# The o projection's four column groups form their products in four ways

## The chip, the cores and the metric

The kernel runs on one core of a Trainium2 chip, as one launch. The metric is the device time of that core in microseconds (us): the median of two runs before the change is 1768.39 us (1767.98 and 1768.80). Lower is better.

## The reference

One layer of a hybrid network works on 128 context tokens and 256 latent tokens, 384 in all, 2048 channels wide. The input projection `h @ w_in` gives q, k, v, an output gate o (1024 channels each), 32 gate columns and a pooling input u. The change touches the product for o alone, and what reads it:

```python
    proj = h @ w_in
    M = MLSTM_WIDTH
    q, k, v, o, g, u = jnp.split(proj, [M, 2 * M, 3 * M, 4 * M, 4 * M + N_GATES * N_HEADS], axis=-1)
    ...
    hm, C, n, m = _mlstm_bidir(q, k, v, gates, C0.astype(f32), n0.astype(f32), m0.astype(f32))
    hm = _rmsnorm(hm, mlstm_norm_w.reshape(N_HEADS, HEAD_DIM)).astype(x.dtype)
    hm = hm.reshape(B, T, M) * jax.nn.sigmoid(o)
    hp = _pool_mixer(u, pool_w, pool_scale, grid_w)
    mix = jnp.concatenate([hm, hp], axis=-1) @ w_out
    x = x + gate_a * _rmsnorm(mix, norm_w[1])
    h = _rmsnorm(x, norm_w[2]) * (1 + scale_f) + shift_f
    y = jnp.square(jax.nn.relu(h @ w1)) @ w2
    x = x + gate_f * _rmsnorm(y, norm_w[3])
```

The conditioning vectors go through a 2048 x 12288 product of their own (adaLN), whose results scale and shift the layers.

## The kernel before

All large products run on TensorE in a rounded 4-byte type, `float32r`, three times each to keep precision. A weight tile is split into a high part `hi` (a copy rounded by ScalarE, L126) and a low part `lo` (the rest, by VectorE, L127), the activations likewise into `xh` and `xl`, and `mm3` (L134 to L137) adds up three products in one PSUM tile: hi with xh, hi with xl, lo with xh. Small products (attention, transposes, adaLN) use plain float32. A PSUM bank is 128 partitions by 512 float32 values, and the kernel has 8 of them, handed out by `bank` (L58).

The program goes through these stages: adaLN for the first norm with the u, v and gate products (up to about 210 us of the profile), the q and k products in four column groups with the attention of one pair of heads behind each, **the o product**, the output projection with `w_out`, and the MLP with `w1` and `w2`, which takes the last 1100 us.

`gemm_T` (L158) forms a transposed product for groups of 256 columns. A group has two PSUM tiles, `acc[g, 0]` and `acc[g, 1]`, of 128 output channels by 384 tokens. The contraction of 2048 runs in four chunks. For each chunk `load_w` starts one 512 KB load from the SP queue and splits it; then come 4 contraction tiles times 2 output tiles times 3 passes, 24 matmuls with 384 tokens as the moving operand and a 128 x 128 weight tile as the stationary one. A group has 96 matmuls. After each chunk the feeds are called: side work in steps, which is a piece of attention (`attention`, L521), of splitting the pooled channels (`split_pool`, L690), or of adaLN on TensorE (`ada1`, `ada_mat`) and on VectorE (`ada2`, `ada_vec`). After the last chunk `evac` reads both PSUM tiles.

For the o product `gemm_T` is called four times, for `w_in` columns 3072, 3328, 3584 and 3840 (L696 to L698), called groups 0 to 3 here. Its `evac_o` (L684) takes the sigmoid of each PSUM tile on ScalarE into a tile named `sig`, and VectorE multiplies the head's output `mix[hd]` by it. The output projection starts right behind, with the groups of columns 0 and 256 sharing four PSUM tiles named `acc_wo`.

The order on each engine comes from a scheduler that keeps the dependences and mostly follows the order of the source. Every matmul instruction comes with a weight load of its own (LDWEIGHTS, engine PEld in the profile). A plain float32 matmul of the source appears as two matmul records in the trace, each with its weight load; a rounded one as one record.

Of the kernel before, what the change touches and what calls it, by code (L numbers as in the profile page):

```python
# [13 lines left out]
P = 128  # L14
D = 2048
KT = D // P
NTOK = 384
NH = 8
M = 1024
# [19 lines left out]
def hymba_kernel(  # L39
# [18 lines left out]
    def bank(name):  # L58
        return psum.tile([P, 512], F32, tag="ps", name=name)

    # ---------------------------------------------------------------- constants and small inputs
    cst = const.tile([P, N_CST, P], F32, name="cst")
# [32 lines left out]

    # silu(c); for every contraction tile in a row of zeros, so that a window of 32 columns puts it in any pair of rows
    cT = const.tile([P, 16, 38], F32, name="cT")
# [7 lines left out]

    # per-channel parameters as columns: prmT [128, 80 | 96]
    prmT = const.tile([P, 176], F32, name="prmT")
# [4 lines left out]

    # ---------------------------------------------------------------- helpers
    def load_w(pieces, name, n=1024, after=(), later=None):
        """pieces: (column offset in the tile view, dram AP [128, a, b]); returns the hi and lo parts."""
        raw = wp.tile([P, 1024], F32, tag="raw", name=f"raw_{name}", bufs=3)
        a = pieces[0][1].shape[1]
        rv = raw[:, 0:n].rearrange("p (a b) -> p a b", a=a)
        for off, src in pieces:
            load_w.ins = nc.sync.dma_start(rv[:, :, off:off + src.shape[2]], src).ins  # L120
        hi = wp.tile([P, 1024], F32R, tag="hi", name=f"hi_{name}", bufs=N_W)
        lo = wp.tile([P, 1024], F32R, tag="lo", name=f"lo_{name}", bufs=N_W)
        with ExitStack() as es:
            for ins in after:
                es.enter_context(tc.issue_after(ins))
            nc.scalar.activation(hi[:, 0:n], raw[:, 0:n], AF.Copy)  # L126
            low = lambda: nc.vector.tensor_tensor(lo[:, 0:n], raw[:, 0:n], hi[:, 0:n].bitcast(F32), op=ALU.subtract)  # L127
            if later is None:
                low()
            else:  # L130
                later.append(low)
        return (hi[:, 0:n].rearrange("p (a b) -> p a b", a=a), lo[:, 0:n].rearrange("p (a b) -> p a b", a=a))

    def mm3(ps, lh, ll, rh, rl, start, stop):  # L134
        nc.tensor.matmul(ps, lh, rh, start=start, stop=False)  # L135
        nc.tensor.matmul(ps, lh, rl, start=False, stop=False)  # L136
        mm3.ins = nc.tensor.matmul(ps, ll, rh, start=False, stop=stop).ins  # L137

    def wview(w):
        return w.rearrange("(k p) n -> p k n", p=P)  # L140

    class Feed:
        """Side work, emitted in steps between the tiles of a large product."""

# [13 lines left out]
    def gemm_T(w, cols, xs, n, evac, feeds=(), korder=(0, 1, 2, 3), name="g", hold=None):  # L158
        """Transposed products: for every 256-column group, out[128 channels, n] in two tiles; groups share the k loop."""
        wv = wview(w)  # L160
        acc = {}
        for g, c0 in enumerate(cols):
            for o in range(2):
                acc[g, o] = bank(f"acc_{name}_{c0}_{o}")
        for ki, kc in enumerate(korder):
            for g, c0 in enumerate(cols):
                hi, lo = load_w([(0, wv[:, 4 * kc:4 * kc + 4, c0:c0 + 256])], f"{name}_{c0}_{kc}", after=hold(ki, g) if hold else ())
                for k in range(4):
                    xh, xl = xs(4 * kc + k)
                    for o in range(2):  # L170
                        mm3(acc[g, o][:, 0:n], hi[:, k, o * P:(o + 1) * P], lo[:, k, o * P:(o + 1) * P],
                            xh[:, 0:n], xl[:, 0:n], ki == 0 and k == 0, ki == 3 and k == 3)
                for f in feeds:
                    f()
        for g, c0 in enumerate(cols):
            for o in range(2):
                evac(c0 // P + o, acc[g, o])
# [7 lines left out]
    def rstd_cols(out, ss, n, scale):  # L185
        """out = (ss * scale + eps) ** -0.5, [128, n]"""
        nc.vector.tensor_scalar(out, ss, scale, EPS, op0=ALU.mult, op1=ALU.add)
        nc.gpsimd.tensor_tensor(out, out, mhalf[:, 0:n], op=ALU.pow)

    def bcast_row(col, name, ps=None):  # L190
        """PSUM tile with [p, 128 i + t] = col[t, i] for every partition p."""
        dg = slot(f"dg_{name}")
        dgv = dg[:, 0:NTOK].rearrange("p (i t) -> p i t", t=P)
        nc.vector.tensor_tensor(dgv, ident.unsqueeze(1).to_broadcast([P, 3, P]), col.unsqueeze(2).to_broadcast([P, 3, P]), op=ALU.mult)
        ps = bank(f"bc_{name}") if ps is None else ps
        nc.tensor.matmul(ps[:, 0:NTOK], ones, dg[:, 0:NTOK], start=True, stop=True)
        return ps

    # ---------------------------------------------------------------- adaLN
    mod = const.tile([P, 6, KT, 2], F32, name="mod")  # L200
    aw = ada_w.rearrange("(p j) n -> p j n", j=16)

    def ada_mat(parts, tags=("ada",)):
        """parts: up to four (i, first channel tile), nk channel tiles each, on the tensor engine.
        Row 32 g + 2 b + (0: ctx, 1: latent) of ps holds part b's sum over the contraction tiles j = g (mod 4)."""
        n, nk = len(parts), parts[0][2]
# [24 lines left out]
    def ada_finish(i, k0, nk, ps):  # L231
        """ps [128, nk, 2]: matrix product columns -> mod[i], with what the channel's norm weight adds to it"""
        v = mod[:, i, k0:k0 + nk, :]
# [10 lines left out]
    def ada_vec(i, q):  # L244
        """512 channels, on the vector engine; the tensor engine adds up the partitions"""
        acc = wp.tile([P, 2, 512], F32, tag="adaacc", name=f"ada_acc_{i}_{q}", bufs=1)
# [27 lines left out]

    # ---------------------------------------------------------------- x: statistics and transposes
    ksteps = [(k, 2) for k in range(0, KT, 2)]
# [45 lines left out]

    # ---------------------------------------------------------------- h, and u, v, gates (token-major), k outermost
    h = []
# [74 lines left out]

    # ---------------------------------------------------------------- pooling mixer  # L400
    mix = [None] * KT
# [22 lines left out]

    # ---------------------------------------------------------------- gate rows, stabilisers
    tokc = ((0, 1, 2), (0, 2, 1))
# [76 lines left out]

    # ---------------------------------------------------------------- q, k and attention
    q_sb, k_sb = [None] * NH, [None] * NH
# [15 lines left out]
    def attention(hp):  # L521
        """Two heads."""
        h0 = 2 * hp
# [44 lines left out]
        def update(i, d, wk):  # L568
            """state after the chunk at token tile i in direction d"""
            out = att.tile([P, 2, 129], F32, tag="C", name=f"C1_{hp}_{i}_{d}", bufs=5)  # L570
# [109 lines left out]

    # ---------------------------------------------------------------- o
    mixs = [None] * KT

    def evac_o(t, ps):  # L684
        hd = t - 24
        s = slot(f"sig{hd}")[:, 0:NTOK]
        nc.scalar.activation(s, ps[:, 0:NTOK], AF.Sigmoid)
        nc.vector.tensor_tensor(mix[hd][:, 0:NTOK], mix[hd][:, 0:NTOK], s, op=ALU.mult)
# [19 lines left out]

    # ---------------------------------------------------------------- output projection
    for k in range(8):  # L710
# [33 lines left out]
    def token_rstd_rows(accs, name, between=None):  # L744
        """PSUM tile with (mean over channels + eps) ** -0.5 of every token, on all partitions"""
        ps = bank(f"tr_{name}")
# [14 lines left out]

    # ---------------------------------------------------------------- gate_f * norm_w[3] as rows
    mlp = ctx.enter_context(tc.tile_pool(name="mlp", bufs=2))
# [12 lines left out]

    # ---------------------------------------------------------------- residual and the MLP's input
    xr = []
# [56 lines left out]

    # ---------------------------------------------------------------- MLP
    hid = {}
# [98 lines left out]
    def done(i, a, b, side=iter(())):  # L936
        """square sum and gate of finished columns, a step of other work in between"""
        jk = mlp.tile([P, 512], F32, tag="jk", name=f"jky{i}_{a}", bufs=1)
# [10 lines left out]
    def residual(i):  # L949
        """norm and residual of a token tile, in pieces"""  # L950
        dst = y_prompt[0] if i == 0 else y_sample[0, (i - 1) * P:i * P]
# [5 lines left out]
    def last_part(ws):  # L957
        """the last 512 columns, token tile by token tile; the last tile in halves"""
        side = iter(())
# [88 lines left out]
```

## Time and profile before

| | |
|---|---|
| median of the runs | 1768.39 us (1767.98 to 1768.80) |
| the profiled execution: span from first to last instruction | 1766.4 us |
| median of the runs less that span | 2.0 us |
| TensorE: busy, matmuls | 1719.2 us (97%), 9643 |
| weight loads: busy | 1539.2 us (87%) |
| VectorE busy | 1067.4 us (60%) |
| ScalarE busy | 627.3 us (36%) |
| moved by DMA | 326.15 MB, 185 GB/s on average |
| the o product: first to last start of its matmuls | 430.2 to 515.7 us |

The profile is one execution, taken by the hardware's profiler. PE is TensorE's matmul unit, PEld its weight load, DVE is VectorE, ACT is ScalarE, POOL is GpSimd, SP the queue that starts most DMAs. [...] What a stream of matmuls costs is the distance from start to start, called a step here, and not the length of a record. The record of a weight load also covers more than the time for which it holds the next one up.

### The profile page before, as it was taken

The page shows a single profiled execution, that of the slowest core. Times are in us where ns is not written, and L with a number is a line of the kernel's source. Part 1 is how long each engine was busy: PE and PEld are TensorE (multiplying, and loading weights), DVE is VectorE, ACT ScalarE, POOL GpSimd, SP SyncE. Part 2 cuts the span into 40 slices and gives each one's busy share as a digit, 9 for nine tenths or more (in the row PEclk, how much of TensorE's full clock was granted, in tenths as well). Part 3 has the DMA queues.
Part 4 walks back from the last instruction along what each step waited for, and adds up shares of the span by engine and source line. Part 5 has one row for each costly group of instructions (what it writes and reads, how often), then busy time and mean ns, then how long its engine had stood idle before and what let it go on. Part 6 is the DMA issues. An engine that isn't in the chain of part 4 may idle for free.

```text
span 1766.4 us, 24738 instructions
## 1 busy us (share of the span) xinstructions
PE 1719.2 (97%) x9643; PEld 1539.2 (87%) x9643; DVE 1067.4 (60%) x1756; ACT 627.3 (36%) x1047; POOL 129.7 (7%) x172
## 2 busy tenths in 40 slices
PE   6999999998999999999999999999999999999997
PEld 3777898887999989988988988988988998998986
DVE  3667877787898849763546644475444443443446
ACT  4322343443434336532432432332332332332332
POOL 0000021222101133110000000000000000000100
PEclk9999999999999999999999999999999999999999
DMA  9888988887777774574345544454434354344543
GB/s 304 279 263 286 299 261 231 253 251 213 232 238 235 237 250 156 185 225 131 120 130 162 175 130 121 130 167 122 129 120 131 120 168 131 120 130 136 165 141 107
DMA packets 250436, 326.15 MB, mean 185 GB/s; under 512 B 14096, under 2 KB 185808, under 8 KB 249936
## 3 DMA queue, kind: packets, MB, share of 16 engines
q1 hardware_dynamic: 242096, 303.74, 54.1%
q0 software_dynamic: 6560, 18.97, 4.3%
q10 hardware_dynamic: 1664, 1.87, 0.3%
q8 instruction: 75, 1.23, 0.3%
q14 instruction: 41, 0.34, 0.1%
HBM read 313.98 MB, written 10.55 MB: 184 GB/s over the span
## 4 chain that ended last, share of the span: by engine, by line
PE 86%; DMA 5%; issue 3%; DVE 2%; POOL 2%; ACT 1%; SPq 0%; ACTq 0%; DVEq 0%; POOLq 0%
PE y L855 10%; PE y L856 10%; PE y L857 10%; PE acc_w L135 9%; PE acc_w L137 9%; PE acc_w L136 9%; DMA ada_raw<-in_ada_w_dram 3%; PE acc_wo L135 3%; PE acc_wo L136 2%; PE acc_wo L137 2%; PE ada L218 2%; PE acc_o L135 1%; PE acc_o L137 1%; PE acc_o L136 1%; PE u L379 1%
## 5 line engine op out<-in xcount | busy, mean ns | idle before, releaser
L127 DVE TENSOR_TENSOR lo_w<-raw_w,hi_w 128x1024 fp32r<-128x1024 f32 x256 | 313.9, 1226 | 440.7 <-ACT hi_w L126 440.3
L126 ACT ACTIVATE hi_w<-raw_w 128x1024 fp32r<-128x1024 f32 x256 | 271.3, 1060 | 666.2 <-PE acc_w L136 302.1
L135 PE MATMUL acc_w<-h2h,hi_w 128*128 128x386 f32 x1024 | 347.8, 341 | 2.4 <-ACT h2h L805 2.4
L137 PE MATMUL acc_w<-h2h,lo_w 128*128 128x386 f32 x1024 | 347.5, 339 | 0.0
L136 PE MATMUL acc_w<-h2l,hi_w 128*128 128x386 f32 x1024 | 347.2, 339 | 0.0
L257 DVE SCALAR_TENSOR_TENSOR ada_acc<-ada_raw,sg,ada_acc 128x512 f32<-128x512 f32 x330 | 237.5, 767 | 21.8 <-DMA ada_raw<-in_ada_w_dram 21.7
L135 PEld LDWEIGHTS acc_w<-h2h,hi_w 128*128 128x128 f32 x1024 | 193.9, 190 | 5.2 <-ACT h2h L805 3.0
L136 PEld LDWEIGHTS acc_w<-h2l,hi_w 128*128 128x128 f32 x1024 | 193.8, 189 | 0.9 <-issue 0.4
L137 PEld LDWEIGHTS acc_w<-h2h,lo_w 128*128 128x128 f32 x1024 | 193.5, 189 | 0.0
L218 PE MATMUL ada<-ada_raw,cT 128*32 128x256 f32 x832 | 61.5, 397 | 5.1 <-DMA ada_raw<-in_ada_w_dram 5.0
L879 DVE TENSOR_TENSOR y<-y,y 128x512 f32<-128x512 f32 x81 | 55.7, 691 | 11.8 <-PE y L857 11.3
L126 ACT ACTIVATE hi_wo<-raw_wo 128x1024 fp32r<-128x1024 f32 x32 | 34.1, 1067 | 67.1 <-PE acc_wo L136 27.9
L846 ACT ACTIVATE z<-z,bz 128x128 f32<-128x128 f32 (+1 forms) x128 | 47.9, 442 | 11.3 <-DVE z L844 11.2
L127 DVE TENSOR_TENSOR lo_wo<-raw_wo,hi_wo 128x1024 fp32r<-128x1024 f32 x32 | 38.7, 1218 | 19.3 <-ACT hi_wo L126 19.3
L379 PE MATMUL v<-hi_v,hh 128*128 128x384 f32 (+1 forms) x144 | 49.0, 341 | 0.0
L381 PE MATMUL v<-hi_v,hl 128*128 128x384 f32 (+1 forms) x144 | 47.2, 328 | 0.0
L380 PE MATMUL v<-lo_v,hh 128*128 128x384 f32 (+1 forms) x144 | 46.9, 326 | 0.0
L774 POOL DMA_DIRECT2D gf_dram<-gfT x1 | 0.5, 519 | 626.8 <-DVE bz L843 626.8
L135 PE MATMUL acc_k<-hh,hi_k 128*128 128x384 f32 x128 | 45.4, 355 | 0.0
L218 PEld LDWEIGHTS ada<-ada_raw,cT 128*32 128x32 f32 x832 | 19.8, 110 | 28.9 <-issue 14.5
L135 PE MATMUL acc_o<-hh,hi_o 128*128 128x384 f32 x128 | 44.7, 349 | 0.0
L135 PE MATMUL acc_q<-hh,hi_q 128*128 128x384 f32 x128 | 44.4, 347 | 0.0
(940 smaller groups left out, 3621.1 us busy)
## 6 DMA issues: line engine op xcount, KB each, us to landing
raw_w<-in_w_dram SPq DMA_DIRECT2D x256, 512.0 KB, 3.7
ada_raw<-in_ada_w_dram SPq DMA_DIRECT2D x192, 512.0 KB, 5.1
raw_wo<-in_w_out_dram SPq DMA_DIRECT2D x32, 512.0 KB, 4.9
raw_u<-in_w_in_dram SPq DMA_DIRECT2D x16, 512.0 KB, 7.4
raw_q<-in_w_in_dram SPq DMA_DIRECT2D x16, 512.0 KB, 5.8
raw_k<-in_w_in_dram SPq DMA_DIRECT2D x16, 512.0 KB, 5.2
raw_o<-in_w_in_dram SPq DMA_DIRECT2D x16, 512.0 KB, 5.3
raw_v<-in_w_in_dram SPq DMA_DIRECT2D x16, 384.0 KB, 7.8
```

The source lines that it names most:

```text
L126: nc.scalar.activation(hi[:, 0:n], raw[:, 0:n], AF.Copy)
L127: low = lambda: nc.vector.tensor_tensor(lo[:, 0:n], raw[:, 0:n], hi[:, 0:n].bitcast(F32), op=ALU.subtract)
L135: nc.tensor.matmul(ps, lh, rh, start=start, stop=False)
L136: nc.tensor.matmul(ps, lh, rl, start=False, stop=False)
L137: mm3.ins = nc.tensor.matmul(ps, ll, rh, start=False, stop=stop).ins
L218: nc.tensor.matmul(ps[32 * g:32 * g + 32, 0:w], cT[:, j, 6 - 2 * b:38 - 2 * b], raw[:, a, :], start=b == 0 and j < 4, stop=b == n - 1 and ...
L257: nc.vector.scalar_tensor_tensor(acc[:, g, :], raw[:, a, :], cj, acc[:, g, :], op0=ALU.mult, op1=ALU.add)
L379: nc.tensor.matmul(acc[i][:, 0:n], xh[:, sl], hi[:, k, :], start=k == 0, stop=False)
L855: nc.tensor.matmul(acc, xh[:, s], hi, start=k == 8 * ch, stop=False)
L856: nc.tensor.matmul(acc, xh[:, s], lo, start=False, stop=False)
L857: nc.tensor.matmul(acc, xl[:, s], hi, start=False, stop=k == 8 * ch + 7)
L879: nc.vector.tensor_tensor(dst, acc[i], dst, op=ALU.add)
```

## The change

The four o groups get four forms. `whole` is what `gemm_T` did, and all other products keep it.

- Group 0 (`parts(192)`): each of the three passes of an output tile is two matmuls of 192 tokens, and each half has a PSUM tile of its own. The group holds 4 banks, not 2, and has 192 matmuls, not 96.
- Group 1 (`split_out`): tokens are addressed as three blocks of 128, on both sides, in one matmul of 384.
- Group 2 (`pass_major`): the three passes are the outer loop and the two output tiles the inner one, so that neighbours write to different banks.
- Group 3 (`parts(128)`): each pass is three matmuls of 128 tokens with a PSUM tile each. The group holds 6 banks and has 288 matmuls.

`evac_o` takes the sigmoid part by part: 14 calls in all, where there were 8. The matmul instructions of the compiled program rise from 9643 to 9931, each with a weight load. The diff also drops comments and doc strings, and lines move by 29 to 32 (`evac_o`'s sigmoid from L687 to L719).

```diff
+    def whole(tiles, xh, xl, n, start, stop):
+        for acc, wh, wl in tiles:
+            mm3(acc[:, 0:n], wh, wl, xh[:, 0:n], xl[:, 0:n], start, stop)
+
+    def parts(w):
+        def f(tiles, xh, xl, n, start, stop):
+            for acc, wh, wl in tiles:
+                for a, b, first, last in ((wh, xh, True, False), (wh, xl, False, False), (wl, xh, False, True)):
+                    for c in range(0, n, w):
+                        mm3.ins = nc.tensor.matmul(acc[c // w][:, 0:w], a, b[:, c:c + w], start=start and first, stop=stop and last).ins
+        return f
+
+    def split_out(tiles, xh, xl, n, start, stop):
+        for acc, wh, wl in tiles:
+            v = lambda t: t[:, 0:n].rearrange("p (a b) -> p a b", a=3)
+            mm3(v(acc), wh, wl, v(xh), v(xl), start, stop)
+
+    def pass_major(tiles, xh, xl, n, start, stop):
+        for first, last in ((True, False), (False, False), (False, True)):
+            for acc, wh, wl in tiles:
+                mm3.ins = nc.tensor.matmul(acc[:, 0:n], wl if last else wh, (xh if first or last else xl)[:, 0:n],
+                                           start=start and first, stop=stop and last).ins
+
+    O_FORMS = {3 * M: parts(192), 3 * M + 256: split_out, 3 * M + 512: pass_major, 3 * M + 768: parts(128)}
+    N_PARTS = {3 * M: 2, 3 * M + 768: 3}
+
+    def form(name, c0):
+        return O_FORMS[c0] if name == "o" else whole
...
-                acc[g, o] = bank(f"acc_{name}_{c0}_{o}")
+                acc[g, o] = [bank(f"acc_{name}_{c0}_{o}_{i}") for i in range(N_PARTS[c0])] if name == "o" and c0 in N_PARTS else bank(f"acc_{name}_{c0}_{o}")
...
-                    for o in range(2):
-                        mm3(acc[g, o][:, 0:n], hi[:, k, o * P:(o + 1) * P], lo[:, k, o * P:(o + 1) * P],
-                            xh[:, 0:n], xl[:, 0:n], ki == 0 and k == 0, ki == 3 and k == 3)
+                    form(name, c0)([(acc[g, o], hi[:, k, o * P:(o + 1) * P], lo[:, k, o * P:(o + 1) * P]) for o in range(2)],
+                                   xh, xl, n, ki == 0 and k == 0, ki == 3 and k == 3)
...
-        nc.scalar.activation(s, ps[:, 0:NTOK], AF.Sigmoid)
+        ps = ps if isinstance(ps, list) else [ps]
+        w = NTOK // len(ps)
+        for i, p in enumerate(ps):
+            nc.scalar.activation(s[:, i * w:(i + 1) * w], p[:, 0:w], AF.Sigmoid)
```

TensorE's queue at the start of group 3, one contraction tile, before. `acc_o_0` and `acc_o_1` are the two PSUM tiles, `hh` and `hl` the tokens' high and low part, `hi_o` and `lo_o` the weights':

```order
L218 MATMUL ada_8_3721<-ada_raw_14_12_4954,cT 32x256 x4
L135 MATMUL acc_o_0_4974<-hh_262,hi_o_0_4978 128x384
L136 MATMUL acc_o_0_4974<-hl_263,hi_o_0_4978 128x384
L137 MATMUL acc_o_0_4974<-hh_262,lo_o_0_4979 128x384
L135 MATMUL acc_o_1_4975<-hh_262,hi_o_0_4978 128x384
```

The same place now, where the third number of `acc_o_0_2` counts the part of the tokens:

```order
L247 MATMUL ada_8_3721<-ada_raw_14_12_5054,cT 32x256 x4
L148 MATMUL acc_o_0_0_5074<-hh_262,hi_o_0_5082 128x128
L148 MATMUL acc_o_0_1_5075<-hh_262,hi_o_0_5082 128x128
L148 MATMUL acc_o_0_2_5076<-hh_262,hi_o_0_5082 128x128
L148 MATMUL acc_o_0_0_5074<-hl_263,hi_o_0_5082 128x128
L148 MATMUL acc_o_0_1_5075<-hl_263,hi_o_0_5082 128x128
L148 MATMUL acc_o_0_2_5076<-hl_263,hi_o_0_5082 128x128
L148 MATMUL acc_o_0_0_5074<-hh_262,lo_o_0_5083 128x128
```

Each matmul of 384 became three of 128 with the same weight tile. Group 0 has the same pattern with two of 128x192; in groups 1 and 2 every row is still a 128x384, in group 2 with the two tiles in turn. Nothing else moves on TensorE: the pieces of attention and adaLN stand between the same chunks as before.

ScalarE's queue around the end of group 2, before. `hi_o` are weight splits of group 3, `sig` the sigmoids of group 2, `ada_sb` a copy for adaLN:

```order
L126 ACTIVATE hi_o_2_5068<-raw_o_2_5066 128x1024
L687 ACTIVATE sig_4968<-acc_o_0_4786 128x384
L126 ACTIVATE hi_o_3_5109<-raw_o_3_5107 128x1024
L223 ACTIVATE ada_sb_8_4960<-ada_8_3721 128x256
L687 ACTIVATE sig_4971<-acc_o_1_4787 128x384
```

The same stretch now:

```order
L126 ACTIVATE hi_o_2_5268<-raw_o_2_5266 128x1024
L126 ACTIVATE hi_o_3_5357<-raw_o_3_5355 128x1024
L252 ACTIVATE ada_sb_8_5060<-ada_8_3721 128x256
L719 ACTIVATE sig_5068<-acc_o_0_4886 128x384
L719 ACTIVATE sig_5071<-acc_o_1_4887 128x384
```

Group 2's first sigmoid now stands behind the last weight split of group 3 and the adaLN copy. The sixth PSUM tile of group 3 (`acc_o_1_2`) reuses the bank which that sigmoid releases, so its first matmul waits for it.

## The prediction

> **What bounds the kernel now.** I read the page first, then the chain of waits and the busy time in the stage that changes. The page says that TensorE is busy nearly all of the span:
>
> ```profile
> span 1766.4 us, 24738 instructions
> PE 1719.2 (97%) x9643; PEld 1539.2 (87%) x9643; DVE 1067.4 (60%) x1756; ACT 627.3 (36%) x1047; POOL 129.7 (7%) x172
> ```
>
> An average over stages doesn't tell what this stage is worth, so next come the busy time of TensorE in the o stage and in the output projection behind it (columns: stretch, length, busy time and records, granted clock, DMA share, GB/s), and the chain of waits in the o stage alone:
>
> ```profile
> core 0: us, PE busy (x), PEclk, DMA share, GB/s
> 430.20:515.90 85.70, 85.70 (x564) 0.99 0.76 245
> 515.90:650.00 134.10, 134.10 (x786) 1.00 0.73 230
> ```
> ```profile
> by line: PE acc_o L135 28.9%; PE acc_o L137 26.3%; PE acc_o L136 26.1%; PE ada L218 6.4%; PE num L589 3.1%; PE num L592 2.1%; PE cu L574 2.1%; PE adav L265 1.2%; PE s L539 1.0%; PE hT L640 0.8%; PE adav L270 0.6%; PE sk L539 0.5%; PE k L543
> ```
>
> TensorE has no idle time from 430.2 to 650 us, the clock is full, and the chain there is TensorE's own queue. So whatever a matmul of this stage costs more goes onto the end, microsecond for microsecond: there is no idle time of TensorE in this stage, or in the 134 us after it, that could swallow it. Loads and splits run ahead of TensorE here, and a later TensorE only gives them slack.
>
> The cost of a matmul in a stream is the step from start to start. Three widths of rounded or plain products give it (timelines of TensorE; first columns are start and length in us):
>
> ```profile
> 443.97 0.34 PE L135 MATMUL acc_o<-hh,hi_o 128*128 128x384 f32 x1
> 444.15 0.33 PE L136 MATMUL acc_o<-hl,hi_o 128*128 128x384 f32 x1
> 444.32 0.34 PE L137 MATMUL acc_o<-hh,lo_o 128*128 128x384 f32 x1
> 444.50 0.34 PE L135 MATMUL acc_o<-hh,hi_o 128*128 128x384 f32 x1
> ...
> 445.37 0.34 PE L137 MATMUL acc_o<-hh,lo_o 128*128 128x384 f32 x1
> ```
> ```profile
> 1752.87 0.28 PE L855 MATMUL y<-hi_w,hid61h 128*128 128x256 f32 x1
> ...
> 1754.06 0.28 PE L856 MATMUL y<-lo_w,hid56h 128*128 128x256 f32 x1
> ```
> ```profile
> 451.16 1.95 PE L574 MATMUL cu<-v,wk 128*128 128x129 f32 x16
> 452.95 1.06 PE L589 MATMUL num<-v,mbc 128*128 128x129 f32 x8
> ```
> ```profile
> 654.35 0.72 PE L750 MATMUL tr_r<-cst,sqa 128*128 128x1 f32 x6
> 654.94 1.48 PE L750 MATMUL tr_r<-cst,sq_mo 128*128 128x1 f32 x12
> 656.35 0.64 PE L218 MATMUL ada<-ada_raw,cT 128*32 128x256 f32 x8
> ```
>
> Rounded, 384 tokens: 8 steps from 443.97 to 445.37, 0.175 us each. Rounded, 256 columns: 10 steps from 1752.87 to 1754.06, 0.119 each. The two are 0.456 and 0.465 ns a column, so down to 256 columns the step is the columns alone. Plain records of 129 columns: 16 in 1.79 us, 0.112 each. Plain records of one column: 18 in 2.00 us, 0.111 each. The last two are the point: one column costs as much as 129. Each of these records loads a full 128 x 128 weight tile, and that load is what remains when the columns are gone. The step is the longer of the columns' time and a floor of 0.112 us, and 256 columns lie just above it.
>
> **The change part by part.** *Group 0.* Before: 96 matmuls by 0.175 = 16.8 us. After: 192 matmuls of 192 tokens. By columns they would take 192 x 0.456 = 0.088 us, under the floor, so I take 0.112: 192 x 0.112 = 21.5 us, which is **+4.7**. The bounds are 0.088 below (then 16.9, nothing lost) and, above, the floor plus the columns, 0.200 (38.4, +21.6). I take the floor because the 129-column rows show the load and the columns side by side and not one behind the other.
>
> *Group 3.* Before 16.8 us. After: 288 matmuls of 128 tokens; by columns 0.058 us, so again the floor, 288 x 0.112 = 32.3 us, **+15.5**. Bounds: 0.058 (nothing lost) and 0.112 + 0.058 = 0.170 (49.0, +32.2). The row nearest in width is the 129-column one, at 0.112; it is of the plain type, though, and no row shows the rounded type under 256 columns. That is the main unknown, and the rivals come from it.
>
> [...]
>
> *Group 1* issues the same 128x384 matmuls, by TensorE's queue, at the same addresses in one run: 0. *Group 2* changes the order of the passes. It loses two neighbours with the same weight tile and gains a change of bank at every matmul. In the rows above L135 to L136 keeps the weight tile (0.18), L136 to L137 changes it (0.17), and L137 to L135 changes the bank as well (0.18): nothing is saved by the one or lost by the other beyond 0.01 us, so 96 matmuls are bounded by -1 and +1 us, and I take 0.
>
> *Six more sigmoids* go to ScalarE, which is busy 36% of the span; they cost the end only where TensorE waits for a bank. That is at two places. The rows of ScalarE around the end of group 2:
>
> ```profile
> 495.05 1.06 ACT L126 ACTIVATE hi_o<-raw_o 128x1024 fp32r<-128x1024 f32 x1 [6.75 <-DMA raw_o<-in_w_in_dram]
> 496.82 0.49 ACT L687 ACTIVATE sig<-acc_o 128x384 f32<-128x384 f32 x1 [0.71 <-PE acc_o L137]
> 497.21 1.05 ACT L126 ACTIVATE hi_o<-raw_o 128x1024 fp32r<-128x1024 f32 x1
> 498.16 0.38 ACT L223 ACTIVATE ada_sb<-ada 128x256 f32<-128x256 f32 x1
> 498.42 0.49 ACT L687 ACTIVATE sig<-acc_o 128x384 f32<-128x384 f32 x1
> ```
>
> Group 2 ends a little before 496.82. Now the split comes first (0.95 until the next starts), then the copy (0.26), then the sigmoid (0.49): the sixth bank of group 3 is free 1.7 us after that end. TensorE first has eight adaLN records between the groups, in the chain of waits this row:
>
> ```profile
> 497.31 0.57 PE ada L218 x8
> ```
>
> Then come 11 short matmuls by 0.112 (1.2), so it needs the bank 1.8 us after that end. So they meet, and the wait is 0 to 0.5. Were the split's load late, as for the one at 495.05, which waited 6.75 us, TensorE would wait for it too: I put 3 us as the upper end. At the start of the output projection the first matmul waits for the first of group 3's six sigmoids; its PSUM tile is complete 1 us before the group ends, so 0 to 0.5 us. Together I take **+0.8**, with 0 and +4 as ends.
>
> *Banks held.* Group 0 holds 4 of 8 and group 3 holds 6, so less is left for the side work: attention's scores and states beside group 0, one adaLN tile and its reduction beside group 3. No row prices this. Before, TensorE waited for none of it (85.70 of 85.70 us busy), so I count nothing beyond the 0.8 and let the 4 us cover it.
>
> **The sum.** 4.7 + 15.5 + 0.8 = 21.0 us on the execution of 1766.4 us: 1787.4. The runs' median lies 2.0 us above that span, so **1789.4 us**, 1.2% slower. Its own range: 480 steps from 0.111 (the one-column rows) to 0.119 (the 256-column rows) give 53.3 to 57.1 us against 33.6, that is 19.7 to 23.5, and with the waits of 0 to 4, 1788 to 1796.
>
> **The rivals.** *The short rounded matmul falls back to the plain type's price.* Plain products take two records each (attention's 8 products `cu` are 16 records), 0.224 us for 129 columns, 1.74 ns a column. If the rounded type is fast only from some width between 192 and 256 columns, which no row excludes, group 3 takes 288 x 0.223 = 64.2 us (+47.4) and group 0 192 x 0.334 = 64.1 (+47.3): 1768.4 + 94.7 = 1863 us. Against it: the 256-column step shows no trace of a rise, and the compiled program has one matmul instruction for each short product. It decides if a 192-token record takes over 0.3 us from start to start.
>
> *The load isn't hidden under a short matmul.* If the next load can begin only late, load and columns add up: 0.200 and 0.170 us, +21.6 and +32.2, with the waits 1768.4 + 54.6 = 1823 us, 3.1% slower. Against it stand the 129-column rows, where 0.112 leaves no room for both; for it, that those columns may be cheap in a way of the plain type that I can't see.
>
> *No floor for the rounded type.* The floor was measured on plain records. If a rounded tile loads faster, the steps shrink with the tokens to 0.088 and 0.058, and the groups take 16.9 and 16.7 us: 1768 to 1773 us with the waits. Against it: the records of rounded and plain weight loads look alike:
>
> ```profile
> L135 PEld LDWEIGHTS acc_o<-hh,hi_o x128: 186/188/334, 430.2 to 515.2; 128*128 128x128 f32 x128
> L750 PEld LDWEIGHTS tr_r<-cst,sqa x6: 188/192/192, 654.2 to 654.8; 128*128 128x128 f32 x6
> ```
>
> [...] The trace has 111 ns where the columns vanish, but of the plain type.
>
> **How the numbers follow.** Forecast 0.62: the floor is seen in two kinds of rows, and the loads look alike. Plain price 0.16, added load 0.11, no floor 0.08; 0.01 for a wait on banks that grows past 35 us, 0.02 for a gain that I don't see. The range has to leave out no more than 2 in 10: it runs from 1768 (no floor) over the forecast to 1825 (added load), which is 0.81, and leaves the plain price out. The likeliest case's own range is 1788 to 1796. A measurement of this kernel tells about 2% from no change, 35.4 us. Slower by more: plain price, added load and the bank waits, 0.28. Within 2%: forecast and no floor, 0.70. Faster: 0.02.
>
> **What would show it.** In the profile after, 128x128 matmuls of `acc_o` should start 0.112 us apart, 128x192 ones as well, and 128x384 ones of groups 1 and 2 0.175 apart. The o stage should last about 106 us in place of 85.7, with TensorE busy throughout, and everything after it should be shifted and else unchanged. A step of 0.06 to 0.09, 0.17 to 0.20, or 0.22 to 0.33 would name the rival that holds. Idle time of PE in front of `acc_o` or `acc_wo` by ScalarE beyond 4 us would make the bank term wrong.

## The result, and the profile after

The changed kernel takes 1792.99 us (two runs, 1791.07 and 1794.91) against 1768.39 before: a ratio of 1.0138, 95% interval 1.0116 to 1.0161, 24.6 us slower. The forecast was 1789.4 us, with 1788 to 1796 as the range of the likeliest case. The total was right; its parts were not all, and most of the runs below are about the part that was missed. One execution below, of the kernel with the moved transposes, was slower at a lower clock (1819.09 us) and is left out of its ratio.

The page of the changed kernel begins so:

```profile
span 1793.1 us, 25314 instructions
PE 1741.5 (97%) x9931; PEld 1562.2 (87%) x9931; DVE 1065.2 (59%) x1756; ACT 628.5 (35%) x1053; POOL 129.3 (7%) x172
```

The 288 matmuls more are there. TensorE's share of 97% has not moved, so this line alone does not say that anything was lost. The busy time of TensorE in the o stage and in the next 134.1 us, over the same stretches of the program as in the prediction:

```profile
431.60:543.40 111.80, 109.61 (x856) 0.96 0.62 198
543.40:677.50 134.10, 134.10 (x785) 1.00 0.70 222
```

From the first matmul of `acc_o` to the first of `acc_wo`, the o stage lasts 111.80 us, where it lasted 86.08 (430.22 to 516.30): +25.7. It begins 1.45 us later (431.67 for 430.22), and all that comes behind it, up to the end of the span, takes 1249.7 us for 1250.1. So the whole loss lies in this stage: 1.45 + 25.72 - 0.47 is the 26.7 us between the two spans. (The medians differ by 24.6; single executions of the kernel before ranged from 1762.9 to 1774.4 us over all runs here.) Two things in the first row were not there before: 2.2 us in which TensorE is idle, and a mean clock of 0.96.

The chain of waits for the stage, and TensorE's waits in it:

```profile
by line: PE acc_o L148 49.2%; DMA ada_raw<-in_ada_w_dram 6.9%; DMA raw_o<-in_w_in_dram 5.2%; DVE ada_acc L286 4.9%; PE acc_o L135 4.1%; PE acc_o L137 3.8%; PE acc_o L136 3.8%; PE ada L247 2.5%; PE num L618 2.2%; DVE lo_o L127 2.0%; ACT mbc 
```
```profile
PE hT L669 <- DVE hs L630: 8.7, 1, 8.7
PE acc_o L148 <- ACT hnT L671: 1.8, 1, 1.8
PE acc_o L148 <- ACT sig L719: 0.3, 1, 0.3
```

L148 is the line of the short matmuls of groups 0 and 3, and has half of the chain. Loads now stand in the chain only since it is followed back through the two new waits on ScalarE, and from there to what ScalarE had waited for; TensorE itself lost 1.8 and 0.3 us by them. The first wait (8.7 us, in columns: total, times, longest) is the idle stretch ahead of the o product, for attention's vector work; it was 8.0 us before.

The steps, from timelines of TensorE (first columns start and length, xN joins neighbours), in the order group 0 late in its run, group 1, group 2, group 3:

```profile
440.96 0.39 PE L148 MATMUL acc_o<-hh,lo_o 128*128 128x192 f32 x2
441.18 0.39 PE L148 MATMUL acc_o<-hh,hi_o 128*128 128x192 f32 x2
```
```profile
466.31 0.34 PE L137 MATMUL acc_o<-hh,lo_o 128*128 128x384 f32 x1
466.49 0.34 PE L135 MATMUL acc_o<-hh,hi_o 128*128 128x384 f32 x1
```
```profile
490.87 0.51 PE L159 MATMUL acc_o<-hh,lo_o 128*128 128x384 f32 x2
491.22 0.52 PE L159 MATMUL acc_o<-hh,hi_o 128*128 128x384 f32 x2
```
```profile
510.89 0.33 PE L148 MATMUL acc_o<-hh,hi_o 128*128 128x128 f32 x1 [0.27 <-ACT sig L719]
511.06 0.50 PE L148 MATMUL acc_o<-hl,hi_o 128*128 128x128 f32 x3
511.39 0.50 PE L148 MATMUL acc_o<-hh,lo_o 128*128 128x128 f32 x3
```

Two matmuls of 192 tokens take 0.22 us, three of 128 take 0.33: 0.11 us each for both widths. Groups 1 and 2 keep 0.175 to 0.18. The row at 510.89 is group 3's wait for its sixth bank. TensorE is idle for 0.27 us there, but from 510.23, where two matmuls start, to 511.06 the starts lose 0.5 us, since the first matmul after this wait also started its successor late (0.17 us, not 0.11).

Group 3's matmuls take 16.62 us in its first two chunks and 8.16 and 8.09 in the others, 32.9 in all, where they took 8.50, 4.36 and 4.31: +15.7, with that 0.5 in it. Group 0's take 16.21, 5.44 and 5.44 for 9.04, 4.29 and 4.30: +9.5, twice what was forecast. All of the surplus lies in its first 96 matmuls. There TensorE's timeline has this:

```profile
432.64 0.63 PE L148 MATMUL acc_o<-hh,lo_o 128*128 128x192 f32 x2
433.07 0.41 PE L148 MATMUL acc_o<-hh,hi_o 128*128 128x192 f32 x1
435.30 0.53 PE L148 MATMUL acc_o<-hh,hi_o 128*128 128x192 f32 x1 [1.81 <-ACT hnT L671]
435.62 0.63 PE L148 MATMUL acc_o<-hl,hi_o 128*128 128x192 f32 x2
436.05 0.63 PE L148 MATMUL acc_o<-hh,lo_o 128*128 128x192 f32 x2
```

and ScalarE's this:

```profile
432.33 2.45 ACT L580 ACTIVATE mbc<-mbc,acol 128x128 f32<-128x128 f32 x8 [0.39 <-DVE mbc L577]
434.68 1.03 ACT L671 ACTIVATE hnT<-hT,prmT 128x384 f32<-128x384 f32 x2
```

The group's fourth bank still holds `hT` of attention's third pair of heads, and the copy `hnT` that reads it stands behind eight exponentials. TensorE stops for 1.81 us after seven matmuls (by the starts it loses 2.1 us). And two matmuls take 0.43 us here, not 0.22: the granted clock is a half. Its course after, and before (last three columns: granted clock, DMA share, GB/s):

```profile
428.00:432.00 4.00, 2.38 (x14) 0.50 0.61 212
432.00:436.00 4.00, 2.19 (x10) 0.50 0.59 162
436.00:440.00 4.00, 4.00 (x21) 0.50 1.07 367
440.00:444.00 4.00, 4.00 (x35) 0.91 0.63 166
```
```profile
428.00:432.00 4.00, 3.84 (x19) 0.58 0.32 101
432.00:436.00 4.00, 4.00 (x25) 1.00 0.83 259
```

In both the clock falls to a half within the idle stretch ahead of the o product: before at 424.6 us, 4.4 us after TensorE's last record had ended, after at 423.6, 2.7 us after it. Before, it is full again 1.2 us into group 0 (half from 424.6 to 431.4); after, only at 440.7, 9 us into it.

One more wait comes between groups 0 and 1: TensorE's next weight load of attention stands behind group 0's additional sigmoids, and that gap is 3.74 us long for 3.34 before.

```profile
464.65 0.52 PEld L618 LDWEIGHTS num<-v,mbc 128*128 128x128 f32 x4 [0.30 <-ACT sig L719]
```

### The profile page after: what moved, and what is told of

Its sections match the earlier page's. It is cut to its first block, busy times and chain, and to the rows that moved or that the text cites. A ratio compares the mean times of both kernels' runs of the same rounds, so it can differ in the third digit from the quotient of the medians.

```text
span 1793.1 us, 25314 instructions
## 1 busy us (share of the span) xinstructions
PE 1741.5 (97%) x9931; PEld 1562.2 (87%) x9931; DVE 1065.2 (59%) x1756; ACT 628.5 (35%) x1053; POOL 129.3 (7%) x172
## 4 chain that ended last, share of the span: by engine, by line
PE 84%; DMA 8%; issue 3%; DVE 3%; ACT 1%; POOL 1%; SPq 1%; ACTq 0%; DVEq 0%; POOLq 0%
PE y L887 10%; PE acc_w L136 10%; PE acc_w L135 10%; PE y L888 10%; PE acc_w L137 10%; PE y L889 10%; DMA ada_raw<-in_ada_w_dram 5%; PE acc_o L148 3%; PE acc_wo L135 2%; PE acc_wo L136 2%; PE acc_wo L137 2%; PE ada L247 2%; PE v L408 1%; PE u L409 1%; PE u L408 1%
## 5 line engine op out<-in xcount | busy, mean ns | idle before, releaser
L127 DVE TENSOR_TENSOR lo_w<-raw_w,hi_w 128x1024 fp32r<-128x1024 f32 x256 | 313.7, 1225 | 441.0 <-ACT hi_w L126 440.7
L247 PE MATMUL ada<-ada_raw,cT 128*32 128x256 f32 x832 | 61.4, 396 | 4.6 <-DMA ada_raw<-in_ada_w_dram 4.6
L137 PE MATMUL acc_q<-hh,lo_q 128*128 128x384 f32 x128 | 44.3, 346 | 2.1 <-DVE lo_q L127 2.1
```

What stands on the lines that cost most here:

```text
L247: nc.tensor.matmul(ps[32 * g:32 * g + 32, 0:w], cT[:, j, 6 - 2 * b:38 - 2 * b], raw[:, a, :], start=b == 0 and j < 4, stop=b == n - 1 and ...
```

## The experiments

Each edit is against the changed kernel unless it says otherwise. Ratios are to the kernel before, run beside it on the same chip (its median was 1769.7 to 1771.1 us there). Where one run is given, the verdict rests on the trace.

**One group at a time.** Three kernels keep one part of the change each, the other groups being `whole` (`N_PARTS`, the number of PSUM tiles, is changed with it).

```diff
-    O_FORMS = {3 * M: parts(192), 3 * M + 256: split_out, 3 * M + 512: pass_major, 3 * M + 768: parts(128)}
+    O_FORMS = {3 * M: whole, 3 * M + 256: whole, 3 * M + 512: whole, 3 * M + 768: parts(128)}
```

> Group 3 alone in 128-token matmuls, groups 0 to 2 as before. Theory A (every matmul costs at least the 0.112 us of its weight load): 288 x 0.112 - 96 x 0.175 = +15.5 us, with a wait of about 0.3 us on a bank at the start of the group, so 1784.2 us. Rival B (part of the extra time of the changed kernel comes from the forms' neighbours, groups 0 to 2, and shows up in group 3): less than +12 us. In the trace 128x128 steps of 0.112 us and no idle time of TensorE beyond 0.5 us in the stage.

Group 3 alone: 1786.55 us, 1.0095 (1.0063 to 1.0128). The o stage is 101.68 us, +15.6, and the step 0.112. The expected wait on a bank did not come: without it group 3's matmuls take 32.4 us, +15.2, and 0.3 of the rest is one stretch more of half clock at the start of group 0 (9.32 us for 9.04).

```diff
-    O_FORMS = {3 * M: parts(192), 3 * M + 256: split_out, 3 * M + 512: pass_major, 3 * M + 768: parts(128)}
+    O_FORMS = {3 * M: parts(192), 3 * M + 256: whole, 3 * M + 512: whole, 3 * M + 768: whole}
```

> Group 0 alone in 192-token matmuls. Theory A alone: 192 x 0.112 - 96 x 0.175 = +4.7 us, 1773.1 us. Theory C (the fourth bank makes TensorE wait 1.8 us for ScalarE's copy of the transposed head, this wait falls behind a stretch in which TensorE idled, and the clock then stays at half for some 10 us more): +4.7 for the matmuls, +1.8 for the wait, +2.5 to 3.1 for the clock, 9 to 10 us in all, 1777.4 to 1778.4 us, with a granted clock of 0.50 until about 440 us in the trace.

Group 0 alone: 1779.17 us, 1.0059 (1.0039 to 1.0079). The o stage is 95.85 us, +9.8, with the same wait and 17.1 us of half clock:

```profile
PE acc_o L148 <- ACT hnT L671: 1.8, 1, 1.8
```

```diff
-    O_FORMS = {3 * M: parts(192), 3 * M + 256: split_out, 3 * M + 512: pass_major, 3 * M + 768: parts(128)}
+    O_FORMS = {3 * M: whole, 3 * M + 256: split_out, 3 * M + 512: pass_major, 3 * M + 768: whole}
```

> Groups 1 and 2 alone in their forms (three blocks of 128 tokens in one matmul; passes outermost over two banks). All theories of the weight load: 0, 1768.4 us, steps of 0.175 us. Rival (a change of bank at every matmul, or the lost neighbour with the same weights, costs 0.01 us or more each): +1 to +2 us.

Groups 1 and 2 alone: 1768.17 us, 0.9988 (0.9973 to 1.0004), no difference that can be told, with steps of 0.175; its o stage of 87.01 us has the clock at a half for one stretch of 3.4 us more than before had (group 0's first half takes 9.94 us for 9.04, in the same form). The three together, 15.6 + 9.8 + 0.9, are the 25.7 us of the whole within a us: the parts add up. This is also the only part of the change that costs nothing.

**The 192-token form in another place.** Group 1 takes it in place of group 0, 24 us behind the idle stretch.

```diff
-    O_FORMS = {3 * M: parts(192), 3 * M + 256: split_out, 3 * M + 512: pass_major, 3 * M + 768: parts(128)}
+    O_FORMS = {3 * M: whole, 3 * M + 256: parts(192), 3 * M + 512: whole, 3 * M + 768: whole}
```

> 192-token matmuls in group 1 in place of group 0, all else as before. Theory C (the wait for the fourth bank and the half clock belong to the place behind the idle stretch): the matmuls' +4.7 us alone, 1773.1 us, granted clock 1.00 through groups 1 to 3. Rival (a 192-token matmul itself costs more than its weight load, as the changed kernel's first half of group 0 suggests with 0.169 us a matmul): +9 to +11 us, 1777 to 1779 us.

1780.14 us, 1.0062 (1.0038 to 1.0087): as much as in group 0. Yet the group's own 192 matmuls take 21.81 us for 17.28, +4.5, at full clock throughout. The rest is a new wait behind it:

```profile
PE acc_o L135 <- DVE mod L268: 4.4, 1, 4.4
```
```profile
485.00:489.00 4.00, 1.84 (x6) 0.57 0.54 166
489.00:493.00 4.00, 4.00 (x16) 0.58 0.66 227
```

Group 1's two additional banks leave group 2 to wait for adaLN on VectorE, by this row for a bank that it still reads, 4.4 us, and the clock falls to a half behind that wait too, which costs group 2's first 48 matmuls 2.3 us more (10.93 for 8.59). So the 4.7 us of the form are confirmed, and the explanation "only the place behind the idle stretch is bad" falls: what the additional banks cost depends on who reads them last, at either place.

**The waits ahead of group 0 moved.** The transposes `hT` of the third pair of heads, with the idle stretch ahead of them, go behind the second chunk of group 0; in a second kernel the same is done to the kernel before.

```diff
-        fa = Feed(attention(g - 1), 1.0)
+        fa = Feed(attention(g - 1, g == 3), 1.0)
...
-        fa.finish()
+        if g < 3:
+            fa.finish()
+    f2 = fa
...
-        gemm_T(w_in, [3 * M + g * 256], hx, NTOK, evac_o, (fa if g < 2 else fs, ada1, ada2), name="o")
+        gemm_T(w_in, [3 * M + g * 256], hx, NTOK, evac_o, ((f2, fa) if g == 0 else (fa,) if g < 2 else (fs,)) + (ada1, ada2), name="o")
```

(In `attention` two steps more stand ahead of the last part for that pair.)

> The changed kernel with the transposes of attention's third pair of heads put behind the second chunk of group 0 in place of ahead of it, so that TensorE has work where it idled for 8.7 us. Theory C (idle time and the wait for the fourth bank hold the clock at half until 440 us): the clock is full or nearly full through group 0, its first 96 matmuls of 192 tokens take 10.8 to 11.5 us in place of 16.2, and the o stage with the transposes in it is 5 to 15 us shorter in sum with the idle time ahead of it; the median falls to 1778 to 1788 us. Rival (the 0.169 us a matmul belongs to the first matmuls of a 192-token group, whatever the clock): those 96 still take about 16 us and only the idle time goes.

> The kernel before with the same move of the transposes and no other change. Theory C: the idle 8 us ahead of the o product and about 1 us of half clock go, unless the adaLN matmul ahead of group 0 waits as long for its load: 1759 to 1764 us. Rival (VectorE is late there anyway and attention's last pair of heads then waits for it in TensorE's queue as long): 1766 to 1769 us.

After with the move: 1787.6 us, 1.0092 (1.0071 to 1.0114). Before with it: 1769.05 us, 0.9993 (0.9983 to 1.0004). In the first, group 0's first 96 matmuls are at full clock without a wait, and take 10.80 us (0.1125 each), not 16.21; so the 192-token form is not slow there by itself. The busy time of that stretch, and TensorE's waits now:

```profile
418.10:428.70 10.60, 10.60 (x99) 1.00 0.84 238
```
```profile
PE k L572 <- ACT hnT L674: 5.5, 1, 5.5
PE hT L672 <- ACT k L547: 1.9, 1, 1.9
```

The idle time is not gone, it stands behind group 0's second chunk, and the half clock with it (48 matmuls there took 8.47 us for 5.44). In the kernel before the move brings nothing either, as the rival had it and not the theory: TensorE waits at other places, 4.1 us for `k` from ScalarE and 2.2 us for `wk` from VectorE. In the two moved kernels `acc_wo` begins at 536.92 and 516.42, 20.5 us apart, where the sum had forecast 21.0. That is near in part by chance, since both kernels have waits and half clock of their own, at different places; by the runs' medians they are 18.6 us apart.

**Only the order within group 0.** Within a chunk, output tile 0 is finished before output tile 1 begins, so the third and fourth bank are needed 48 matmuls later. Nothing else moves.

```diff
-                for k in range(4):
+                first = name == "o" and c0 == 3 * M
+                for os_, k in [((o,), k) for o in range(2) for k in range(4)] if first else [((0, 1), k) for k in range(4)]:
                     xh, xl = xs(4 * kc + k)
-                    form(name, c0)([(acc[g, o], hi[:, k, o * P:(o + 1) * P], lo[:, k, o * P:(o + 1) * P]) for o in range(2)],
+                    form(name, c0)([(acc[g, o], hi[:, k, o * P:(o + 1) * P], lo[:, k, o * P:(o + 1) * P]) for o in os_],
```

> As after, but group 0 finishes output tile 0 within a chunk before output tile 1, so its third and fourth PSUM tiles are needed 48 matmuls (5 us or more) later. Theory (the wait for the fourth tile and the two clock windows that it broke are what group 0 cost beyond 4.7 us): no wait of 1.8 us on the copy hnT, full clock a window or two earlier, the first 96 matmuls 11 to 13 us instead of 16.2, the o stage 107 to 109 us instead of 111.8, the time 1.0104 to 1.0125 of before, where after has 1.0138. Rival (the 192-token matmuls are slow by themselves in their first 96, or the wait moves to another tile): the first 96 again take about 16 us, the o stage 111 to 112 us, 1.0138.

1.0122 (1.0086 to 1.0158), an interval too wide to tell it from after. The trace does tell: the wait on `hnT` is gone, the first 96 matmuls take 13.97 us (16.21 in after, 10.80 at full clock), and the o stage 109.39 us. That lies between theory and rival, and just beyond both of the theory's ranges (11 to 13, 107 to 109). What it missed is the clock. Three stretches of 3.4 us, which the expectation calls windows (the half clock lasts for multiples of 3.41 us in these traces), and behind them the same of the kernel with group 3 alone, which has 384 tokens there:

```profile
430.80:434.20 3.40, 3.40 (x19) 0.50 0.55 169
434.20:437.60 3.40, 3.40 (x18) 0.50 0.91 303
437.60:441.00 3.40, 3.40 (x33) 1.00 0.98 297
```
```profile
426.30:429.70 3.40, 3.40 (x18) 0.50 0.38 111
429.70:433.10 3.40, 3.40 (x21) 0.99 0.76 234
```

With 384 tokens the clock was full behind one busy stretch. With 192 tokens it took two, without an idle moment on TensorE. The kernel with the late `hT` shows the same (busy at half clock from 439.9 to 446.7). In after itself, one stretch was enough once the wait was over. In both kernels that needed two, the first stretch began with side work, so that it held fewer of the group's matmuls. These alone, in the first two stretches above:

```profile
430.76:434.17 3.41, 3.27 (x15) 0.50 0.55 171
434.17:437.58 3.41, 3.41 (x18) 0.50 0.90 300
```

All nine traces that have a stretch at half clock filled by 192-token matmuls alone (18 records) are at full clock behind it; the stretches with 15 and 14 were not enough. Why is open.

The wait is then worth 16.21 less 13.97, 2.2 us: what it costs by the starts, and little more. Most of the clock's loss (13.97 less 10.80 is 3.2 us) came also without it, so the theory, which put two of the half-clock stretches down to the wait, fails in that part. How the stretches fall matters too: in the other traces of this group 0 its first 96 matmuls take 15.3 to 16.8 us.

**Is the floor the weight load?** In group 3 each matmul keeps its 128 tokens and loads a weight tile of 64 columns, half of the channels.

```diff
-                        mm3.ins = nc.tensor.matmul(acc[c // w][:, 0:w], a, b[:, c:c + w], start=start and first, stop=stop and last).ins
+                        mm3.ins = nc.tensor.matmul(acc[c // w][0:m, 0:w], a[:, 0:m], b[:, c:c + w], start=start and first, stop=stop and last).ins
```

> The changed kernel with weight tiles of 64 columns in group 3 in place of 128, as many matmuls, 128 tokens each; half of the group's output channels aren't computed, the other half's gates are used for them. Theory A1 (the floor is the weight load and goes with its columns): steps fall to 0.058 to 0.062 us, where the tokens' own time takes over, group 3 takes 17 to 18 us, the span is 14 to 15 us shorter than the changed kernel's. Theory A2 (the floor is one per instruction pair, whatever the size): steps stay at 0.112 us and the span stays.

1779.52 us (one run). The step falls from 0.112 to 0.061 us, here three rows of three matmuls, 0.19 and 0.18 us behind one another:

```profile
522.16 0.35 PE L148 MATMUL acc_o<-hl,hi_o 128*64 128x128 f32 x3
522.35 0.34 PE L148 MATMUL acc_o<-hh,lo_o 128*64 128x128 f32 x3
522.53 0.35 PE L148 MATMUL acc_o<-hh,hi_o 128*64 128x128 f32 x3
```

0.061 is about what 128 tokens cost by the columns (128 x 0.456 ns is 0.058). Half the load, and the floor is out of the way. (The cut also halves the rows that each matmul writes to PSUM; no run has the one without the other. Group 3 takes 18.9 us, a little over the forecast, as its wait for the sixth bank grew to 1.1 us.)

**Half of the tokens.** The other operand is cut: 64 of the 128 tokens of each matmul, with the full weight tile.

```diff
-                        mm3.ins = nc.tensor.matmul(acc[c // w][:, 0:w], a, b[:, c:c + w], start=start and first, stop=stop and last).ins
+                        mm3.ins = nc.tensor.matmul(acc[c // w][:, 0:m], a, b[:, c:c + m], start=start and first, stop=stop and last).ins
```

> The changed kernel with its 128-token matmuls of group 3 cut to the first 64 tokens of each block; the gates of the other 64 tokens aren't computed, the first ones' are used for them. Theory A (a floor per matmul, set by its weight load): steps stay at 0.112 us, group 3 at 32.3 us, the span within 2 us of the changed kernel's. Rival (cost by tokens with a fixed part, for instance 0.058 us of tokens and 0.054 us besides): steps of 0.083 us, group 3 at 24 us, the span 8 us shorter.

1823.25 us (one run), 30 us more than after, for half of the group's work. No theory had that. The stretches of group 3's matmuls:

```profile
509.20:512.50 3.30, 3.30 (x34) 1.00 1.00 327
512.60:536.00 23.40, 23.40 (x112) 0.50 0.36 120
537.80:553.00 15.20, 15.20 (x73) 0.50 0.11 34
554.40:569.60 15.20, 15.20 (x72) 0.50 0.46 139
```

TensorE is busy all the time, and still the clock drops to a half 3.3 us after the group begins, and stays there for 61.4 us, until the 384-token matmuls of the output projection have run for a while. At full clock, in the first 3.3 us, the step is 0.11, so the floor is as expected; at half clock it is 0.214 (15.38 us for 72), 1.9 times the 0.112 of full clock. Three runs look for what decides it: tokens and channels both 64, 96 tokens with the full tile, and 128 tokens with 32 channels.

> Left out: in group 3 each matmul has only the first 64 of its 128 tokens and only 64 of its 128 channels, so gates of half the tokens and half the channels are not computed (the others' stand in their place). With 64 tokens and 128 channels the granted clock fell to 0.50 for 61 us and the step was 0.214 us; with 128 tokens and 64 channels the clock was full and the step 0.061. [...] Rival V (short matmuls of 64 tokens throttle it whatever the load): half clock for most of the group, a step of about 0.11 us, the group 30 to 33 us, the o stage about 112 us.

> Left out: in group 3 each matmul has only the first 96 of its 128 tokens, so the gates of the last 32 of every 128 tokens are not computed (those of the first 32 stand in their place). The weight load is the full 128 columns. Theory of the floor: the step is still 0.112 us at full clock, 288 matmuls take 32.3 us, the o stage is that of after, 111 to 112 us. [...]

> Left out: in group 3 each matmul has only 32 of its 128 channels (all 128 tokens), so the gates of three quarters of the channels are not computed (the first 32 stand in their place). So far the clock stayed full with 128 tokens by 128 channels (0.112 us) and 128 by 64 (0.061), and fell to 0.50 with 64 by 128, 64 by 64 and 96 by 128. Theory W (what counts is the work in the array, tokens times channels for the time: 0.44 of the array at least where it stayed full, 0.36 at most where it fell): 32 channels are under a quarter of the array, so the clock falls to 0.50 for most of the group, the step is about 0.115 us, the 288 matmuls take 31 to 34 us and the o stage 110 to 114 us. Rival V (a matmul of fewer than 128 tokens lets the clock fall, whatever its channels): full clock, a step of 0.056 to 0.062 us, the columns alone, 16 to 18 us and an o stage of 96 to 99 us. A step of 0.03 us would mean that the columns are not the bound at 128 tokens.

The edits are the ones above with other numbers. A stretch of each group 3, in this order:

```profile
521.00:528.00 7.00, 7.00 (x68) 0.50 0.77 236
```
```profile
513.80:537.00 23.20, 23.20 (x111) 0.50 0.33 114
```
```profile
519.80:524.00 4.20, 4.20 (x73) 1.00 0.94 290
```

| tokens x channels in group 3 | step, us | granted clock | time of the run, us |
|---|---|---|---|
| 128 x 128 (the changed kernel) | 0.112 | full | 1792.99 |
| 128 x 64 | 0.061 | full | 1779.52 |
| 128 x 32 | 0.060 | full | 1790.46 |
| 96 x 128 | 0.214 | half, for 61.4 us | 1823.99 |
| 64 x 128 | 0.214 | half, for 61.4 us | 1823.25 |
| 64 x 64 | 0.107 | half, for 34.1 us | 1800.81 |

Theory W, tokens times channels over time, falls with 128 x 32 (by the steps of 0.061 and 0.112 us and 0.456 ns a column, its shares 0.44 and 0.36 are 0.48 and 0.39, an estimate): 128 times 32 in 0.060 us is 68 a ns, and the clock stays full, where 64 x 128 with 73 and 96 x 128 with 110 (both in 0.112 us, before the clock fell) lost it. Another account would be the share of the time in which tokens go through the array. With 64 x 64 the step was 0.058 us at full clock, so that this share is 0.50 (64 columns of 0.456 ns, an estimate), close to the 0.52 of 128 x 128, and yet the clock fell. But that run doesn't settle it, since the stretch in which the clock fell holds a wait of 1.2 us for the sixth bank:

```profile
513.80:517.50 3.70, 2.48 (x43) 1.00 1.02 348
```

So two accounts are left. One is the rival, matmuls of fewer than 128 tokens. The other is a count of tokens over time, here estimated from the steps: at full clock 1.14 tokens a ns (128 x 128) kept the clock, 0.86 (96 x 128) and 0.57 (64 x 128) lost it; at half clock 0.90 (192 tokens in 0.213 us) and 1.2 (384 in 0.32) brought it back, 0.60 (64 x 64) and less did not. No run here tells them apart, and what in the chip counts is open. (The 128 x 32 kernel is slower than the one with 64, as its output projection waited 7.2 us for adaLN on VectorE.)

## Why the prediction was right

**TensorE's queue is the bound, and the loss goes onto the end.** Right: 25.7 us in the stage, and the time behind it unchanged to 0.5 us.

**The floor of 0.112 us.** Right for both widths, though it was taken from plain records: 0.112 to 0.113 at 192 and at 128 tokens. That it belongs to the weight load had been argued from records of one column and of 129; the 64-column tile showed it, as far as the load can be told from the rows written. The rivals that differ from it only in this number (0.223 to 0.334, 0.170 to 0.200, 0.058 to 0.088) are all excluded. At half clock it was 0.214 us (15.38 us for 72 matmuls of 64 tokens).

**Group 3, +15.5.** Measured +15.2 for the form (32.4 us for 17.2, in group 3 alone), and 0.5 for the sixth bank in the trace of after (forecast 0 to 0.5).

**Groups 1 and 2, nothing.** Right: 0.9988, with 1 in its interval.

**Group 0, +4.7.** As the price of the form this is right: +4.5 in group 1, and 21.7 us for 17.1 (+4.6) when each chunk is taken from a trace in which it ran at full clock. But group 0 cost +9.5. The step that failed is "Banks held": "No row prices this. Before, TensorE waited for none of it (85.70 of 85.70 us busy), so I count nothing beyond the 0.8 and let the 4 us cover it." A full row of busy time shows that two banks a group could be had in time; it says nothing on the third and fourth. The sign that was to show a wrong bank term, idle time beyond 4 us, did not come either: TensorE's matmuls idled for 2.1 us, and the rest of the loss is in the clock. The surplus of 9.5 over the kernel before divides so, from the 10.80 and 8.50 us that the first two chunks take at full clock: 4.6 for the form, 1.8 for the wait, and 3.1 for the clock (3.6 in after, 16.21 less 10.80 and 1.81, against 0.5 before, 9.04 less 8.50). The last was in no term. By the kernel that takes group 0 tile by tile the 4.9 us divide otherwise: 2.2 come with the fourth bank, and 2.7 are a loss to the clock that is there without any wait. So the stage lost 25.7 where the sum said 21.0: 4.9 more for the fourth bank and the clock, 0.4 less for the two forms (4.6 and 15.2, not 4.7 and 15.5), and 0.1 more for the other waits (0.5 at the sixth bank and 0.4 for attention's weight load behind the sigmoids, which the sum did not name, for 0.8); 0.1 is left over.

**The clock.** The prediction read "the clock is full" off a row with a mean of 0.99 over 85 us. That mean hid 1.2 us at half clock at the group's start, which is where the group was sensitive. In the traces the half clock lasts for stretches that are multiples of 3.41 us (3.4, 6.8, 10.2, 13.7, 17.1). Group 0 begins at half clock, since the clock fell in the idle time ahead of it, but a shorter stop went with a loss too: in the kernel with 64 tokens group 0 had full clock when its wait for the fourth bank came, and lost it again behind a stretch that was busy for 1.44 us of 3.40.

```profile
434.00:437.40 3.40, 1.44 (x13) 1.00 0.71 208
437.40:440.80 3.40, 3.40 (x19) 0.50 1.08 382
```

Nor was a busy TensorE enough to keep the clock or to bring it back: behind the first busy stretch at 192 tokens, in the two kernels that needed two, it was still a half, and the runs with 64 and 96 tokens and a full weight tile lost it without idle time (3.30 of 3.30 and 3.60 of 3.60 us busy ahead of the fall). What sets it is open.

**The range.** The range reached 6.6 us above the forecast, 3.2 of it for waits and the rest for a longer step. That room, meant for other things, took in 4.9 us that were not foreseen: that the total fell into the range is partly luck.

## What to carry to other kernels

Price a short matmul by the longer of its columns and its weight load: with a full 128 x 128 tile that was 0.112 us here, so that 384 tokens in one instruction cost 0.175, in two 0.224 and in three 0.336. A product that holds more PSUM banks needs, for each of them, the last reader of the tile that was there, and that reader's place in its engine's queue; a trace in which nothing waits says nothing on banks that were not asked for. Behind an idle stretch read the granted clock in steps of a few us, not over a stage, since a stop can cost the clock as well: the 4.4 us that group 2 waited, with the 192-token form in group 1, cost it 2.3 us more.

## What the runs showed of the hardware that had not been expected

- With matmuls of 64 or 96 tokens, issued without a gap, the granted clock fell to a half for as long as they ran and some us beyond (61.4 us, 18 stretches of 3.41), and with 64 tokens and half a weight tile, where the group began with a wait of 1.2 us, it was a half for 34.1 us. With 128 tokens it stayed full, whether 128, 64 or 32 channels were used. The 128 tokens of group 3 stand on the good side of it: 96 tokens took 0.214 us where 128 took 0.112. Whether the width of a matmul counts or the tokens per time is open.
- Behind a stretch of 3.4 us with a wait of 2.0 us in it, the full clock was a half for the next stretch (64 tokens, group 0 at 434.0).
- At half clock the 192-token step is 0.213 us and the 64-token one 0.214, 1.9 times the floor at full clock; 384 tokens took 0.32 us for 0.175, 1.8 times.
- After an idle stretch, 192-token matmuls needed two busy stretches of 3.4 us to get the clock back in two kernels (tile by tile, late `hT`), the first of them not filled by these matmuls alone, and one in the seven kernels in which group 0 waits for its fourth bank; 384-token ones needed one each time.
